# Second layer's experts: slots and gathers of the second and third unit moved ahead of ordering the experts

## The chip, the cores and the metric

The kernel runs on one core of one Trainium2 chip. The number that counts is the device time of one execution in microseconds. Before the change it is 1020.47 us, the median of three runs (1019.87 to 1021.63).

The core has five instruction queues that run side by side and wait for each other through semaphores. PE is the matmul engine (TensorE), DVE the vector engine, ACT the scalar engine, POOL the GpSimd engine. SP issues most of the transfers from the chip's memory (HBM). Each queue runs its instructions strictly in the order in which they stand.

## The reference, cut to what matters

Two layers over 256 latent tokens of width 1024, with 256 context tokens beside them in the first. Each layer ends in a mixture of 16 experts, of which every token takes two, chosen within one of four groups:

```
out = zeros
for e in range(16):
    hid = silu(h @ w_gate[e]) * (h @ w_up[e])      # 1024 -> 512
    out = out + combine[:, e] * (hid @ w_down[e])  # 512 -> 1024
h = h + m[5] * out
```

The change touches only the experts of the second layer, the last part of the program. There each expert's three matrices are 2 MB each in fp32, and all 16 experts' weights are read: 96 loads of 1 MB.

## The kernel before, in words

A token goes to two experts of 16, so the kernel does not push all 256 tokens through every expert. Experts are worked through in *units*. A pair unit holds two experts with 64 slots each, a solo unit one expert with 128 slots. In the second layer `PLAN[1] = "PPSPSPPPP"`: nine units, of which the first, second, fourth and the last four are pairs. In a pair the two experts' matmuls run in two halves of the array's columns in plain fp32 (`L919`); a solo unit's weights are split into a high and a low part (`whi` on ACT, `L171`; `wlo` on DVE or POOL, `L175`) and multiplied in three products (`L504` to `L506`).

`FIXED[1] = 5`: the first five experts keep their places, and they fill units 1, 2 and 3. The other eleven are put in order of how many tokens chose them. `order` (`L946` on) counts tokens per expert, makes the permutation `perm`, and writes `ids`, the experts' numbers in their new order. SP reads these into registers (`L296`) before it can load weights of the experts with open places. `arrange` (`L970` on) then permutes the tokens' ranks and weights with small PE transposes and products (`L976` to `L994`).

Three steps make the input of a unit:

- `slots1(n)`: DVE compares the ranks of tokens with slot numbers (`sgm`, `L1606`), PE multiplies this with token numbers and weights (`L1610`), and DVE reads from the product the tokens' numbers (`sli`, `L1612`, `L1614`) and weights (`slw`, `L1618`).
- `gather1(n)`: POOL starts an indirect DMA (`L1624`) that fetches the rows of these tokens from memory into `xg`. Two buffers exist (tag `H1`). They are also the buffers of `f`, the normalised tokens; the first gather can overwrite one only after all its readers are through.
- `xpose1(n)`: PE transposes `xg` (`L1638`) into PSUM, ACT and DVE copy it into `xh` (`L1644`). For the first unit alone there is no gather: PE multiplies `f` with the slots (`L1641`).

Then come `gu("g")` and `gu("u")`, 16 matmuls each for a pair unit, `hidden`, `hid_T` (`L1020`), `down1` (16 more) and `combine1` (`L1667`). In the code before, `slots1(0)` and the first unit's input come first, then `order`, the first gate products, `arrange`, the slots and gathers of units 2 and 3, and then the loop over the units.

Weights come through a ring: at this stage 13 buffers of 1 MB. A load goes out when its buffer is free: after the last matmul on it in a pair unit, after its split in a solo unit. SP issues all loads from one queue, in a fixed order, so a load that waits holds up those behind it. The order of loads is gate of unit n, down of unit n-1, up of unit n.

PSUM tiles of the tag `tr` (transposes, slot products, small products) have two buffers, so each new one waits for the readers of the one before the last.

The order of instructions on each engine is not the order of the code. A list scheduler with a timeline model of its own places them, so an edit in one place can move instructions that it does not name, also far behind it. The readings of the order below are from the built programs.

Of the kernel before, what the change touches and what calls it, by code (L numbers as in the profile page):

```python
# [24 lines left out]
FIXED = (2, 5)  # L25
# [182 lines left out]
def backbone(ctx: ExitStack, tc: tile.TileContext, I, out):  # L208
# [19 lines left out]
    def tr_t():  # L228
        return psum.tile([128, 512], F32, name="tr", tag="tr", bufs=2)
# [278 lines left out]
    def split(hi, lo, x, eng):  # L508
        i = S.activation(hi, x, AF.Copy)  # L509
        eng.tensor_sub(lo, x, hi.bitcast(F32))  # L510
        return i
# [435 lines left out]
    def order(l, pool, nch, oh):  # L947

        pk = tr_t()
        for c in range(nch):  # L950
            T.matmul(pk[0:16, 0:16], one[:, 0:16], oh[:, c], start=(c == 0), stop=(c == nch - 1))
        t16 = lambda n, name: pool.tile([16, n], F32, name=name, tag=name)
        key, kd, kc, place, over, cap = t16(16, "key"), t16(16, "kd"), t16(1, "kc"), t16(1, "place"), t16(1, "over"), t16(1, "cap")
        V.scalar_tensor_tensor(key, pk[0:16, 0:16], 32.0, kb[l], op0=OP.mult, op1=OP.add)
        V.tensor_mul(kd, key, idt[0:16, 0:16])
        V.tensor_reduce(kc, kd, axis=AX.X, op=OP.add)
        V.tensor_scalar(kd, key, kc, None, op0=OP.is_ge)
        V.tensor_reduce(place, kd, axis=AX.X, op=OP.add)
        perm = t16(16, "perm")
        V.tensor_scalar(perm, ior[0:16, 0:16], place, None, op0=OP.is_equal)  # L960
        pt = tr_t()
        T.matmul(pt[0:1, 0:16], eid[0:16], perm, start=True, stop=True)
        V.tensor_copy(ids[l], pt[0:1, 0:16])
        V.tensor_mul(kd, perm, caps[l])
        V.tensor_reduce(cap, kd, axis=AX.X, op=OP.add)
        V.tensor_scalar(over, kc, kbe[l], 1.0 / 32, op0=OP.subtract, op1=OP.mult)
        V.tensor_sub(over, over, cap)
        return perm, cap, over
# [125 lines left out]
    with phase("moe0") as mp:  # L1094
# [17 lines left out]
        def id_weights(name, cw, n):  # L1112

            t = mp.tile([128, 4, n, 4], F32R, name=name)
            for j in (0, 3):
                V.tensor_copy(t[:, :, :, j], idk[:, :, None].to_broadcast([128, 4, n]))
            V.tensor_copy(t[:, :, :, 1], cw[:, :, 0:n])
            V.tensor_sub(t[:, :, :, 2], cw[:, :, 0:n], t[:, :, :, 1].bitcast(F32))
            return t

        ranks, idw = pm, id_weights("idw2", comb, 2)
        units = UNITS[0]
# [187 lines left out]
    with phase("odd") as op:  # L1310
# [190 lines left out]
        units = [(b, c) for b in range(2) for c in range(4)]  # L1501
# [78 lines left out]
    with phase("moe1") as mp:  # L1580
# [5 lines left out]
        units = UNITS[1]  # L1586
# [12 lines left out]
        def slots1(n):  # L1599

            u = units[n]
            w = 128 // len(u)
            sg = mp.tile([128, 2, 128], F32, name="sgm", tag="sgm", bufs=2)
            for c in range(2):
                for h, p in enumerate(u):
                    V.tensor_scalar(sg[:, c, h * w:h * w + w], ior[:, 0:w], ranks[:, c, p:p + 1], None, op0=OP.is_equal)  # L1606
            pw_ = tr_t()
            m = 2 * len(u)
            for c in range(2):
                T.matmul(pw_[:, 0:m], sg[:, c], idw[:, c, u[0]:u[0] + len(u)].rearrange("p e j -> p (e j)"),  # L1610
                         start=(c == 0), stop=(c == 1))
            V.tensor_scalar(sli[0:w, n:n + 1], pw_[0:w, 1:2], OFF, None, op0=OP.add)  # L1612
            if len(u) == 2:
                V.tensor_scalar(sli[w:128, n:n + 1], pw_[w:128, 3:4], OFF, None, op0=OP.add)  # L1614
            t = mp.tile([128, 1], F32, name="slw1", tag="slw1", bufs=4)
            for h in range(len(u)):
                hs = slice(h * w, h * w + w)
                V.tensor_copy(t[hs], pw_[hs, 2 * h:2 * h + 1])  # L1618
            slw[n] = t
            return sg  # L1620

        def gather1(n):
            xg[n] = cp.tile([128, D], F32, name=f"xg{n}", tag="H1", bufs=2)
            return G.indirect_dma_start(out=xg[n], out_offset=None, in_=fd1,  # L1624
                                        in_offset=bass.IndirectOffsetOnAxis(ap=sli[:, n:n + 1], axis=0),
                                        bounds_check=255, oob_is_err=False)

        def xpose1(n, sg=None):

            xh = mp.tile([128, KD, 128], F32R, name="xh1", tag="xh", bufs=2)  # L1630
            xl = mp.tile([128, KD, 128], F32R, name="xl1", tag="xl", bufs=1) if len(units[n]) == 1 else None
            for hf in range(2):
                pt = tr_t()
                for q in range(4):
                    ks = slice((hf * 4 + q) * 128, (hf * 4 + q) * 128 + 128)
                    o = pt[:, q * 128:(q + 1) * 128]
                    if sg is None:
                        T.transpose(o, xg[n][:, ks], idt)  # L1638
                    else:
                        for c in range(2):  # L1640
                            T.matmul(o, f1[c][:, ks], sg[:, c], start=(c == 0), stop=(c == 1))  # L1641
                fs = slice(hf * 4, hf * 4 + 4)
                if xl is None:
                    (V.tensor_copy if hf else S.copy)(xh[:, fs].bitcast(F32).rearrange("p k t -> p (k t)"), pt)  # L1644
                else:
                    split(xh[:, fs], xl[:, fs], pt.rearrange("p (k t) -> p k t", k=4), V)
            xT[n] = (xh, xl)
# [23 lines left out]
        st.more(1, lambda: Two(x_t("wa", "X"), x_t("wb", "X")))  # L1671
        st.load()
        idw = id_weights(comb)
        xpose1(0, slots1(0))
        perm, cap, over = order(1, mp, 2, oh)
        st.limit = st.upto = 1 << 30
        st.load()
# [1 line left out]
        pg = gu("g", 1, 0, *xT[0])  # L1679
        ranks, combS, ranksT = arrange(1, mp, 2, perm, pm, comb, "amt")  # L1680
        idw = id_weights(combS)
        for n in (1, 2):
            slots1(n)
            gather1(n)
        reg = any_over(mp, over)
# [137 lines left out]
```

## Time and profile before

| what | us |
|---|---|
| median of three runs | 1020.47 |
| profiled execution | 1022.2 |
| its span, first to last instruction | 1020.4 |
| PE busy in the span | 943.5 |
| DVE, POOL, ACT busy | 538.9, 351.0, 342.2 |

In the span PE works 92% of the time, at a mean granted clock of 0.963 of full speed. The second layer's experts take from about 737 us to the end. The profile's page cuts the span into 40 slices; in the last nine the transfers move between 326 and 387 GB/s, except in the very last. Just ahead of them stand slices with less (250 and 157). A listing of instructions in order of time has: start, duration, engine, line, operation, output and inputs, tiles used on PE, shape, count, and in brackets how long the engine sat idle before it and what ended this. Two records of PE stand for one fp32 matmul instruction.

### The profile page before, as it was taken

Reading aid. Unit: us, or ns where it says so; the run is one execution under the profiler, and the core shown is the slowest. Engines: PE = TensorE matmul, PEld = TensorE weight load, DVE = VectorE, ACT = ScalarE, POOL = GpSimd, SP = SyncE. Lnnn points to the kernel's source line nnn. Section 1 sums busy time; section 2 is a strip of 40 time slices with the busy share of each in tenths; the row PEclk is TensorE's granted clock in tenths of the full one; section 3 lists DMA queues with packets and bytes.
Section 4 is the critical chain, followed back from the end, with each engine's and each line's share of the span. In section 5 each row is a group of like instructions: output and inputs, shape, how many; then the busy total and the mean of one; then the engine's idle time right before and its main releaser. Section 6 shows DMA issues by size and latency. Waiting matters only on the chain. (4 is left out here: it accounts for less than half of the span.)

```text
span 1020.4 us, 12766 instructions
## 1 busy us (share of the span) xinstructions
PE 943.5 (92%) x4686; PEld 589.3 (58%) x4686; DVE 538.9 (53%) x931; ACT 342.2 (34%) x492; POOL 351.0 (34%) x244
## 2 busy tenths in 40 slices
PE   4999999988899999999999798999796999999995
PEld 2677677746675678558756577466553444643331
DVE  3552425286783777457935683648523464532223
ACT  3421113144563266236534362433201132410001
POOL 2351103235552746524823533023001242443112
PEclk9999999998899999999999999899985999999998
DMA  9964668948699799799599772495496899999993
GB/s 311 363 241 145 213 254 296 350 166 291 217 320 375 248 344 356 251 359 387 203 385 384 255 266 86 123 335 182 157 346 250 326 387 383 387 382 386 386 386 130
DMA packets 149316, 296.28 MB, mean 290 GB/s; under 512 B 6776, under 2 KB 17032, under 8 KB 149112
## 3 DMA queue, kind: packets, MB, share of 16 engines
q1 hardware_dynamic: 143080, 278.06, 76.3%
q0 software_dynamic: 6128, 17.26, 4.6%
q8 instruction: 40, 0.66, 0.3%
q14 instruction: 36, 0.29, 0.1%
q10 hardware_dynamic: 32, 0.01, 0.0%
HBM read 295.97 MB, written 4.24 MB: 294 GB/s over the span
## 5 line engine op out<-in xcount | busy, mean ns | idle before, releaser
L171 ACT ACTIVATE whi<-w 128x1024 fp32r<-128x1024 f32 x182 | 190.6, 1058 | 225.8 <-PE mm L506 93.2
L175 POOL TENSOR_TENSOR wlo<-w,whi 128x1024 fp32r<-128x1024 f32 x64 | 163.5, 2555 | 260.7 <-ACT whi L171 218.4
L175 DVE TENSOR_TENSOR wlo<-w,whi 128x1024 fp32r<-128x1024 f32 x118 | 178.4, 1524 | 95.8 <-ACT whi L171 94.9
L919 PE MATMUL mm<-w,xh 128*64 128x512 f32 x632 | 162.9, 607 | 0.5 <-DMA w<-in_moe_w_up_dram 0.5
L515 POOL TENSOR_TENSOR H<-H,am 128x512 f32<-128x512 f32 x68 | 95.6, 1423 | 146.9 <-DVE am L514 144.5
L919 PEld LDWEIGHTS mm<-w,xh 128*64 128x64 f32 x632 | 48.7, 139 | 90.9 <-issue 87.4
L504 PE MATMUL mm<-whi,xh 128*128 128x512 f32 x192 | 79.6, 414 | 2.4 <-DVE am L514 1.6
L505 PE MATMUL mm<-wlo,xh 128*128 128x512 f32 x192 | 78.8, 410 | 2.7 <-DVE wlo L175 2.3
L506 PE MATMUL mm<-whi,xl 128*128 128x512 f32 x192 | 78.0, 406 | 0.0
L919 PE MATMUL yp<-w,hh 128*64 128x512 f32 x288 | 74.0, 606 | 0.8 <-DVE hh L1023 0.8
L514 DVE TENSOR_TENSOR am<-mm,m5b 128x512 f32<-128x512 f32 x68 | 45.7, 684 | 30.6 <-PE mm L1221 19.5
L1221 PE MATMUL mm<-y,seT 128*128 128x512 f32 x208 | 54.5, 397 | 0.2 <-ACT y L509 0.2
L504 PE MATMUL mm<-aTh,whi 128*128 128x512 f32 x128 | 52.4, 416 | 2.1 <-ACT aTh L665 2.1
L505 PE MATMUL mm<-aTl,whi 128*128 128x512 f32 x128 | 51.7, 404 | 0.0
L506 PE MATMUL mm<-aTh,wlo 128*128 128x512 f32 x128 | 51.3, 402 | 0.0
L1221 PEld LDWEIGHTS mm<-y,seT 128*128 128x128 f32 x208 | 38.1, 188 | 15.4 <-issue 4.9
L919 PEld LDWEIGHTS yp<-w,hh 128*64 128x64 f32 x288 | 23.0, 140 | 41.0 <-issue 39.4
L504 PEld LDWEIGHTS mm<-whi,xh 128*128 128x128 f32 x192 | 37.4, 195 | 14.6 <-issue 4.7
L505 PEld LDWEIGHTS mm<-wlo,xh 128*128 128x128 f32 x192 | 37.5, 195 | 14.4 <-DVE wlo L175 3.4
L432 PE MATMUL yp<-w,sT 128*32 128x512 f32 x288 | 45.2, 642 | 0.0
L506 PEld LDWEIGHTS mm<-whi,xl 128*128 128x128 f32 x192 | 37.5, 195 | 7.8 <-DVE xl L510 0.3
L510 DVE TENSOR_TENSOR yl<-yp,yh 128x512 fp32r<-128x512 f32 x16 | 11.0, 690 | 58.4 <-ACT yh L509 58.4
(362 smaller groups left out, 1546.3 us busy)
## 6 DMA issues: line engine op xcount, KB each, us to landing
w<-in_moe_w_gate_dram SPq DMA_DIRECT2D x61, 1024.0 KB
w<-in_moe_w_up_dram SPq DMA_DIRECT2D x58, 1024.0 KB
w<-in_moe_w_down_dram SPq DMA_DIRECT2D x57, 1024.0 KB
w<-in_ada_w_dram SPq DMA_DIRECT2D x48, 1024.0 KB
w<-in_even_w_in_dram SPq DMA_DIRECT2D x8, 1024.0 KB
w<-in_odd_w_in_dram SPq DMA_DIRECT2D x5, 1024.0 KB
w<-in_even_w_out_dram SPq DMA_DIRECT2D x4, 1024.0 KB
s4b<-mrow SPq DMA_DIRECT2D x6, 512.0 KB
```

Of the source, the lines that this page charges most:

```text
L171: self.nc.scalar.activation(hi, t, AF.Copy)
L175: eng.tensor_sub(lo, t, hi.bitcast(F32))
L432: T.matmul(pa[32 * j:32 * j + 32, :], s_at(s * 4 + j, u), t[:, j, :], start=first and s == 0, stop=last and s == 1, skip_group_check=True)
L504: T.matmul(o, lh, rh, start=first, stop=False)
L505: T.matmul(o, lh, rl, start=False, stop=False)
L506: T.matmul(o, ll, rh, start=False, stop=last)
L510: eng.tensor_sub(lo, x, hi.bitcast(F32))
L514: V.tensor_mul(t, pp, m)
L515: eng.tensor_add(acc, acc, t)
L919: T.matmul(o[hs], xh[:, kk, hs].bitcast(F32), w[h][:, k], start=first and k == 0, stop=last and k == 3, skip_group_check=True)
L1221: marks["comb"] = T.matmul(pp, seT[n][:, c * 128:(c + 1) * 128], t[:, hs], start=(i == 0), stop=(i == 2 * len(ns) - 1))
```

## The change

The slots of unit 2 are computed right after those of unit 1, ahead of the first unit's transposed input; its gather follows that input. Slots and gather of unit 3 come next. Both take the ranks as they are before the permutation (`pm`, `comb`), which for experts with fixed places are the same numbers. Only then come `order`, the first gate products and `arrange`. Units 2 and 3 are left out of the later loop, which has nothing more to do here. `FIXED[1]` is 5 and unit 3 ends with expert 4, so `ahead` is `[1, 2]`.

```diff
         idw = id_weights(comb)
-        xpose1(0, slots1(0))
+
+        ahead = [n for n in (1, 2) if units[n][-1] < FIXED[1]]
+        sg0 = slots1(0)
+        slots1(1)
+        xpose1(0, sg0)
+        gather1(1)
+        for n in ahead[1:]:
+            slots1(n)
+            gather1(n)
         perm, cap, over = order(1, mp, 2, oh)
         st.limit = st.upto = 1 << 30
         st.load()
...
         ranks, combS, ranksT = arrange(1, mp, 2, perm, pm, comb, "amt")
         idw = id_weights(combS)
-        for n in (1, 2):
+        for n in range(1 + len(ahead), 3):
             slots1(n)
             gather1(n)
         reg = any_over(mp, over)
```

In the built program the order differs from the start of this stage on, and there are no more and no fewer instructions of these steps. First place, PE at the stage's start: the slot products (`L1610`) and the first unit's input (`L1641`); `f_6203` and `f_6320` are the two halves of the tokens.

```order
-L1610 MATMUL tr<-idw_6431,sgm 128x4
+L1610 MATMUL tr<-idw_6431,sgm 128x4 x4
 L1641 MATMUL tr<-sgm,f_6203 128x128
-L1610 MATMUL tr<-idw_6431,sgm 128x4
 L1641 MATMUL tr<-sgm,f_6320 128x128
 L1641 MATMUL tr<-sgm,f_6203 128x128
```

Unit 2's two slot products now stand ahead of the first unit's input, which waits for DVE's reading of unit 1's product; unit 3's two stand behind that input, ahead of the first gate matmul. Second place, PE between the last up product of unit 1 and the first gate product of unit 2 (`L980` to `L994` are `arrange`, `L1034` and `L1007` the overflow flag and the ranks' transposes, `L1638` the transposed input of unit 2):

```order
 L980 MATMUL tr<-perm,pmT 128x16 x2
 L985 MATMUL tr<-idt,comb 16x128 x2
 L990 MATMUL tr<-perm,cbT 128x16 x2
 L994 MATMUL tr<-pmT,perm 16x256
-L1610 MATMUL tr<-idw_6540,sgm 128x4 x2
-L1610 MATMUL tr<-idw_6540,sgm 128x2 x2
 L1034 MATMUL tr<-idt,over 1x16
 L1007 MATMUL tr<-pmST,idt 64x256 x2
-L1638 MATMUL tr<-idt,xg_6556 128x128 x8
-L1610 MATMUL tr<-idw_6540,sgm 128x4 x2
+L1638 MATMUL tr<-idt,xg_6481 128x128 x8
+L1610 MATMUL tr<-idw_6570,sgm 128x4 x2
```

Four slot matmuls are gone from here; the two of unit 4, which need the permuted ranks, still stand between unit 2's input and its first gate matmul. On ACT, in the same place, the copy of unit 2's input now comes ahead of the split of unit 3's first gate weights, and the second split further back:

```order
 L1013 ACTIVATE sg<-mm 128x512
-L171 ACTIVATE whi<-w 128x1024 x2
 L1644 COPY xh_6646<-tr 128x512
 L171 ACTIVATE whi<-w 128x1024 x2
 L1013 ACTIVATE sg<-mm 128x512
-L509 ACTIVATE yh_6708<-yp 128x512 x2
+L509 ACTIVATE yh_6708<-yp 128x512
+L171 ACTIVATE whi<-w 128x1024 x2
+L509 ACTIVATE yh_6708<-yp 128x512
```

The copy no longer stands behind work that waits for a transfer. DVE has the same turn: its copy of that input now precedes the low parts `wlo`. Third place, SP: the loads that follow the first load of unit 3's gate, before the change,

```order
L142 DMA w<-in_moe_w_gate_dram 128x4x512 [waits DMAHW2_49,DMAHW1_49,DVE_49]
L142 DMA w<-in_moe_w_down_dram 128x4x512 [waits DMAHW2_49,DMAHW3_49,DVE_49,Pool_49]
L142 DMA w<-in_moe_w_down_dram 128x4x512 [waits DMAHW4_49,PE_49]
L142 DMA w<-in_moe_w_down_dram 128x4x512 [waits DMAHW5_49,PE_49]
L142 DMA w<-in_moe_w_down_dram 128x4x512 [waits DMAHW6_49,PE_49]
L142 DMA w<-in_moe_w_up_dram 128x4x512 [waits DMAHW7_49,PE_49]
```

and now:

```order
L142 DMA w<-in_moe_w_down_dram 128x4x512 [waits DMAHW2_49,PE_49]
L142 DMA w<-in_moe_w_down_dram 128x4x512 [waits DMAHW3_49,PE_49]
L142 DMA w<-in_moe_w_down_dram 128x4x512 [waits DMAHW4_49,PE_49]
L142 DMA w<-in_moe_w_gate_dram 128x4x512 [waits DMAHW5_49,DMAHW1_49,DVE_49]
L142 DMA w<-in_moe_w_up_dram 128x4x512 [waits DMAHW6_49,PE_49]
L142 DMA w<-in_moe_w_down_dram 128x4x512 [waits DMAHW7_49,PE_49]
```

Three of unit 2's down loads, which wait for PE (the first two for the first half of unit 2's gate products, the third for their second half), now stand ahead of unit 3's second gate load, which waits for the split of its first one (the DVE semaphore); the fourth down load no longer waits for a split. Ten of the eleven register reads of `ids` and that of the overflow flag stand right ahead of these loads in one run; before, they were spread between loads. Behind this, SP's order is soon the same again. Later on PE differs in places as well: unit 3's down products now stand inside unit 4's up products, unit 4's down products come earlier within unit 5's up products, and in the last unit two of the four final combining matmuls (`L1722` before, `L1730` now) stand inside the last down products.

## Rows read from the trace of the kernel before

**Rows 1.** Busy time of each engine in stretches, with granted clock, DMA share, GB/s.

```profile
core 0: us, PE busy (x) PEld busy (x) DVE busy (x) ACT busy (x) POOL busy (x), PEclk, DMA share, GB/s
775.00:780.00 5.00, 1.94 (x8) 1.56 (x8) 0.00 (x0) 0.14 (x1) 0.00 (x0) 0.50 0.67 244
780.00:785.00 5.00, 2.61 (x8) 1.46 (x10) 3.96 (x10) 2.34 (x3) 0.11 (x1) 0.50 0.08 22
785.00:790.00 5.00, 5.00 (x18) 1.50 (x16) 0.28 (x2) 1.53 (x2) 1.22 (x2) 0.62 0.70 263
790.00:795.00 5.00, 5.00 (x25) 1.84 (x22) 2.59 (x1) 0.48 (x1) 2.02 (x1) 1.00 0.12 14
795.00:1000.00 205.00, 197.31 (x886) 91.15 (x886) 83.13 (x125) 40.58 (x56) 64.47 (x44) 0.98 1.04 386
...
1001.00:1002.00 1.00, 1.00 (x8) 0.34 (x6) 0.00 (x0) 0.00 (x0) 0.00 (x0) 1.00 0.15 55
```

**Rows 2.** PE in order of time at the stage's start.

```profile
742.29 0.77 PE L1641 MATMUL tr<-sgm,f 128*128 128x128 f32 x2
742.86 0.43 PE L1610 MATMUL tr<-idw,sgm 128*128 128x4 f32 x2
...
765.44 0.61 PE L980 MATMUL tr<-perm,pmT 16*128 16x16 f32 x4
...
766.87 0.61 PE L990 MATMUL tr<-perm,cbT 16*128 16x16 f32 x4 [0.51 <-DVE cbT L987]
...
768.70 1.84 PE L1610 MATMUL tr<-idw,sgm 128*128 128x4 f32 x8 [0.69 <-DVE idw L1595]
...
771.59 1.12 PE L1007 MATMUL tr<-pmST,idt 16*64 16x256 f32 x4 [0.85 <-DVE ovs L1036]
777.51 1.94 PE L1638 MATMUL tr<-idt,xg 128*128 128x128 f32 x8 [4.81 <-DMA xg<-fd,sli]
782.39 1.01 PE L1610 MATMUL tr<-idw,sgm 128*128 128x4 f32 x4 [2.94 <-ACT xh L1644]
783.34 12.37 PE L919 MATMUL mm<-w,xh 128*64 128x512 f32 x42
```

**Rows 3.** POOL in order of time: the first of the gathers.

```profile
770.85 1.13 POOL L1624 DMA_INDIRECT xg<-fd,sli  x1 [32.51 <-PE tr L1034]
```

**Rows 4.** SP in order of time, two rows of its loads.

```profile
783.34 0.38 SPq L142 DMA_DIRECT2D w<-in_moe_w_gate_dram  x1
793.17 2.93 SPq L142 DMA_DIRECT2D w<-in_moe_w_down_dram  x4
```

**Rows 5.** DVE in order of time: compares of unit 1's slots, and a cast of `arrange`.

```profile
741.31 0.74 DVE L1606 TENSOR_SCALAR sgm<-cst,posm 128x64 f32<-128x64 f32 x4
...
768.05 0.41 DVE L996 CAST pmST<-tr 16x256 fp32r<-16x256 f32 x1
```

**Rows 6.** ACT in order of time: the copy of unit 2's input.

```profile
781.77 0.57 ACT L1644 COPY xh<-tr 128x512 f32<-128x512 f32 x1
```

**Rows 7.** PE later in the stage: unit 3's slots and first wait; unit 4's gate.

```profile
811.91 0.50 PE L1610 MATMUL tr<-idw,sgm 128*128 128x2 f32 x4
...
821.58 0.50 PE L505 MATMUL mm<-wlo,xh 128*128 128x512 f32 x1 [2.32 <-DVE wlo L175]
...
839.07 9.66 PE L919 MATMUL mm<-w,xh 128*64 128x512 f32 x42
```

**Rows 8.** The stretches of 1 us in which the granted clock changes.

```profile
768.00:769.00 1.00, 0.31 (x3) 0.33 (x2) 0.50 (x2) 0.00 (x0) 0.00 (x0) 0.68 1.03 381
...
788.00:789.00 1.00, 1.00 (x4) 0.24 (x2) 0.00 (x0) 0.53 (x1) 0.00 (x0) 0.58 0.62 246
```

**Rows 9.** PE in order of time: the last down products and what follows.

```profile
999.32 7.09 PE L919 MATMUL yp<-w,hh 128*64 128x512 f32 x32 [0.78 <-DVE hh L1023]
1006.34 3.70 PE L1722 MATMUL mm<-yb,sgT 128*128 128x512 f32 x8
```

**Rows 10.** DVE in order of time at the end.

```profile
1003.02 0.69 DVE L1719 TENSOR_TENSOR yb<-yp,m5b 128x512 f32<-128x512 f32 x1 [3.76 <-PE yp L919]
...
1010.87 1.72 DVE L1713 TENSOR_TENSOR hg<-H,gfb 128x512 f32<-128x512 f32 x1
```

## The prediction

> **What bounds the kernel now.** I read the busy time by stretches first, because a share over the whole span hides stages. From 795 to 1000 us PE is busy for 197.31 of 205 us and the transfers run at 386 GB/s [rows 1]: PE and the weight stream are both nearly full, and the loop over the units has little room. Just ahead of it stands a hole in both. From 775 to 795 us the transfers move 244, 22, 263 and 14 GB/s [rows 1]; against 386 that is (142 + 364 + 123 + 372)/386 x 5 = 13.0 us of stream time lost. Second, PE in order of time tells why [rows 2]. Unit 1's up products end where the first row of `arrange` begins, at 765.44. Unit 2's gate begins at 783.34. In these 17.9 us PE does small products and waits: 4.81 us for unit 2's gathered rows, 2.94 us for the copy of its input. The gather was issued at 770.85 [rows 3], 5.4 us after PE had run out of matmuls, because its slots stood behind `arrange`. Third, SP [rows 4]: one gate load of unit 3 at 783.34, nothing until 793.17. So PE's gap, and the loads tied to it, are what this change can reach. At the end the stream is through in the stretch 1001 to 1002 (55 GB/s [rows 1]), while the second half of the last down products, which needs the last load, starts at 999.32 + 7.09/2 = 1002.9 [rows 9]. PE sets the end, and the stream has only about 1.9 us in hand.
>
> **The head: +1.3 us.** Unit 2's slots now stand ahead of unit 1's input. DVE does four more compares (0.74 us [rows 5]). PE runs its slot product of 0.43 us at once, but unit 1's first input product, which before started at 742.29 beside this [rows 2], takes over the PSUM buffer of unit 1's slots and must wait until DVE has read them. That reading started only when PE had done the second slot product at 742.86 + 0.43 = 743.29; now it can start when the compares are done, near 742.8, and its four tiny reads take about 0.7 us (an estimate from the 0.74 us for four compares). So the input starts near 743.55, 1.26 later, less the 0.43 us that no longer stand inside it. Behind it come unit 3's two slot products, 0.50 us at full clock [rows 7]. 1.26 - 0.43 + 0.50 = 1.3. Bounds: 0.5 if only the two products count; 2.5 if they run at half clock (0.86) and the clock's rise moves back by a microsecond too. Unit 1's 32 matmuls follow back to back; `order`'s three products only stand at other places between them. Its chain on DVE has 16 matmuls as cover and needs a tenth of that.
>
> **The gap: -10.8 us.** What is left between 765.44 and unit 2's gate, with the old durations. `arrange` ends at 768.70 - 0.69 = 768.01, as before. `L1007` needs the cast `pmST`, through at 768.05 + 0.41 = 768.46 [rows 5]; it takes 1.12, to 769.6. The transposes of unit 2's input are next, 1.94, to 771.55: their gather now goes out when unit 1's input has been read (sixteen matmuls from 743.55, at 0.43 each like the slot product: 750.4) and has 19 us, where it took 777.51 - 770.85 = 6.66 [rows 2, 3]. The wait of 2.94 goes too. ACT copied that input at 781.77 [rows 6], behind the splits of unit 3's weights, which wait for a transfer. Now the copy stands ahead of them, and its 0.57 us lie beside the second half of the transposes (0.97). Unit 4's slots add 0.95 (783.34 - 782.39). Gate 2 starts at 772.5: the gap is 7.1 instead of 17.9. Bounds: 9 us, if copies and semaphores cost 2 us more than these rows show; 5.5, if it all runs at full clock (the half-clock durations 1.12, 1.94 and 0.95 then nearly halve). I take 7.1, whose rows are the nearest. What is late next is `arrange`, whose result unit 4's slots need.
>
> **The clock: -1.4 us.** The granted clock falls in the stretch from 768 and comes back in that from 788 [rows 8]; in between it is 0.50, 1.2 GHz. Unit 2's 42 records take 12.37 us then, and 9.66 at full clock in unit 4 [rows 2, 7], so half clock costs 2.7 there. Before the fall PE had only the gaps of 0.51 and 0.69 us [rows 2], which stay; before the rise it had worked without a break from 782.39. In the changed kernel PE is at work without a break from `L1007` on, about 4 us ahead of gate 2, so I expect a fall and a rise inside unit 2, and take half: 1.4, bounds 0 and 2.7.
>
> The Trainium skill (TensorE: Matmul & The Clock Gate, HAM oscillation) lets the half rate come back when PE sits idle for long, as in waits for transfers. By that rule the short gaps that stay would keep the full rate, and both terms would be at their best. The trace disagrees so far: the clock fell at 768 after gaps of 0.51 and 0.69 us.
>
> **The weight stream: 0.** Were PE alone ahead, the stream would catch it. It shifts too. Unit 2's down loads wait for PE, gate 2's first half, no longer behind two splits in a row. Unit 3's first gate load is the last of eight; it landed near 778, where the stream went dry (244 of 386 GB/s fill 3.2 of the 5 us from 775), and lands no later now, since the gathers' two times 0.5 MB have moved out of its way. Gate 2 starts at 772.5 + 1.3 = 773.8. Its first half is 16 of the 42 records, 3.7 us at full clock and twice that at half: 777.5 to 781.2. First data come 1.3 us after an issue (22 GB/s from 780 to 785 is 0.3 us' worth, behind the issue at 783.34). So the hole is 1 to 4.5 us instead of 13, and the gain of 8.5 to 12, with the 1.9 in hand, covers PE's 10.9 but for half a microsecond at worst. The eleven register reads on SP lie in the same wait: they cost nothing unless they take over 10 us.
>
> **The end: +1.0 us.** Two of the last four combining matmuls, 3.70/4 = 0.925 each [rows 9], now stand inside the last down products, one matmul into their second half. They need `yb`, ready at 1003.02 + 0.69 = 1003.71 [rows 10], when PE is at 1003.3: 0.4 wait and 1.85 work. The last down product then ends 2.25 later; its `yb` (0.69) and two matmuls (1.85) follow, where before all but 0.1 of `yb` was covered and four matmuls stood (3.70). 2.25 + 0.6 + 1.85 - 3.70 = +1.0 for the last matmul. DVE's last product, 1.72 where its like take 0.69 [rows 10], may shrink: bounds 0 and 1.3.
>
> **The middle: 0.** Unit 3's and unit 4's products are interleaved otherwise. The nearest row is PE's wait of 2.32 for a low part [rows 7]; two such, gained or lost, bound it at 4.6 both ways. I find none that the new order makes certain.
>
> Sum: +1.3 - 10.8 - 1.4 + 1.0 = -9.9. Made against the profiled execution, 1022.2 us with 1.8 around its span of 1020.4, this is 1012.3; the median of the runs lies 1.7 below that execution, so I predict 1010.6.
>
> **Rivals.** *The clock holds through the gap*: 5.5 instead of 7.1, 2.7 instead of 1.4, head 1.0: 1.0 - 12.4 - 2.7 + 1.0 = -13.1, 1007.4. For it: PE's pauses shrink from 10 us to about 1. Against it: the fall at 768 came ahead of the long waits.
>
> *The stream takes over*: the hole stays at 8 us, because gate 2's first half comes at half clock and SP's reads and second-gate load add to it. Then the stream gains 5.0, the 1.9 in hand makes 6.9, the end costs 1.0: -5.9, 1014.6. For it: 386 GB/s over 205 us leaves nothing to catch up with. Against it: only the first two loads need PE's first half, and at 1.05 MB each they bridge the next 5.4 us.
>
> *It does not do what it says*: unit 4's slots still need `arrange`, and they stand ahead of gate 2. If that chain were what ends last, the gap would stay and head and end cost 2.3; with half of the two long waits left (3.9) it comes out at 1018.9. Against it: `arrange` ended at 768.01, 9.5 us before the gather came.
>
> *Slower*: unit 3's second gate load now stands behind three loads that wait for PE. It would go out near 785 (783.34 before), while unit 3 is due 10.9 us earlier, at 801.5 (its slots ended at 812.4 [rows 7]). From that issue to the next load, which waited for the split, it took 9.8 us [rows 4]; with two loads of 2.7 ahead its split ends near 800. From 801.5 on each microsecond costs at most one, and past 812 the kernel is slower; that takes four more loads ahead of it, or a split stuck as long on ACT behind unit 1's down outputs. Price: 1024.
>
> **How the numbers follow.** Forecast 0.60, clock holds 0.12, stream 0.18, no gain 0.05, slower 0.05. A difference under 0.2% (2 us) could not be told from none. The first three are all faster: 0.90; same 0.05; slower 0.05. The forecast's own bounds, head +1.2, gap +1.9, clock +1.4 and the middle, which partly cancel, give 1007 to 1014. The range reaches a little past the clock's case and past the stream's: 1006.0 to 1015.8.
>
> **What would show it.** Right: unit 2's transposes without a wait for the gather; its gate about 7 us after unit 1's up products end; the copy ahead of the splits; transfers below 300 GB/s for under 5 us between 770 and 795; the span's end near 1010.5. Wrong: a new wait of several microseconds at unit 2's input or unit 3's second half, transfers dry past 785, or PE waiting for loads in the last units.

## The result, and the profile after the change

The changed kernel took 1014.45 us (median of 13 runs, 1009.77 to 1019.41) beside 1021.42 us for the kernel before (13 runs). The ratio is 0.9939, with a 95% interval of 0.9921 to 0.9956: 6.2 us faster, 4.5 to 8.1. The forecast was 9.9 us faster and 1010.6 us. The direction was right and the time lies in the range; the forecast gain was 3.7 us too large.

The profiled execution took 1016.73 us, with a span of 1014.9. Its last stage starts 2.14 us later than in the profile before (first product at 742.18, before at 740.04). Nothing of the change stands ahead of that place, so I compare times from the stage's start. First PE in order of time, against [rows 2]:

```profile
744.01 1.84 PE L1610 MATMUL tr<-idw,sgm 128*128 128x4 f32 x8 [0.83 <-DVE sgm L1606]
745.85 5.83 PE L1641 MATMUL tr<-sgm,f 128*128 128x128 f32 x32
751.51 0.51 PE L1610 MATMUL tr<-idw,sgm 128*128 128x2 f32 x4
751.95 6.22 PE L919 MATMUL mm<-w,xh 128*64 128x512 f32 x26
...
767.62 0.61 PE L980 MATMUL tr<-perm,pmT 16*128 16x16 f32 x4
...
769.05 0.61 PE L990 MATMUL tr<-perm,cbT 16*128 16x16 f32 x4 [0.50 <-DVE cbT L987]
...
770.70 1.11 PE L1007 MATMUL tr<-pmST,idt 16*64 16x256 f32 x4 [0.34 <-DVE pmST L996]
771.75 1.97 PE L1638 MATMUL tr<-idt,xg 128*128 128x128 f32 x8
773.53 1.02 PE L1610 MATMUL tr<-idw,sgm 128*128 128x4 f32 x4
774.48 11.08 PE L919 MATMUL mm<-w,xh 128*64 128x512 f32 x42
```

The gap from `L980` to unit 2's gate is 774.48 - 767.62 = 6.86 us, where it was 17.90. The transposes (`L1638`) and the product behind them carry no bracket: neither the gathered rows nor the copy are waited for. ACT's copy now stands ahead of the split that waits for a transfer:

```profile
772.90 0.58 ACT L1644 COPY xh<-tr 128x512 f32<-128x512 f32 x1 [8.94 <-PE tr L1638]
783.32 2.01 ACT L171 ACTIVATE whi<-w 128x1024 fp32r<-128x1024 f32 x2 [9.83 <-DMA w<-in_moe_w_gate_dram]
```

Next the same kernel in stretches (columns as in [rows 1]), with the place where its transfers now slacken and the end of the stream:

```profile
775.00:780.00 5.00, 5.00 (x20) 1.55 (x18) 1.00 (x6) 0.00 (x0) 1.00 (x1) 0.76 1.05 385
780.00:785.00 5.00, 5.00 (x24) 1.74 (x20) 0.60 (x1) 1.69 (x2) 0.00 (x0) 1.00 0.97 349
785.00:790.00 5.00, 5.00 (x26) 1.77 (x25) 2.45 (x3) 0.92 (x2) 0.00 (x0) 1.00 0.99 345
790.00:795.00 5.00, 5.00 (x24) 1.52 (x22) 1.14 (x2) 0.00 (x0) 0.00 (x0) 1.00 1.02 367
...
885.00:890.00 5.00, 5.00 (x23) 1.66 (x22) 2.57 (x3) 3.43 (x4) 2.58 (x2) 1.00 0.91 342
890.00:895.00 5.00, 5.00 (x21) 3.68 (x21) 2.88 (x3) 2.15 (x3) 2.67 (x1) 1.00 0.50 159
...
994.00:995.00 1.00, 1.00 (x6) 0.27 (x2) 0.36 (x1) 0.00 (x0) 0.00 (x0) 1.00 0.21 78
```

The hole of 13.0 us at the stage's start has shrunk to (37 + 41 + 19)/386 x 5 = 1.3 us. A smaller one, (44 + 227)/386 x 5 = 3.5 us, has appeared at 885 to 895, where SP waits 10.1 us for the low part of a solo unit before it can issue the next load. The stream is through near 994.2; PE reads the last load from 997.30 on:

```profile
990.94 4.51 PE L919 MATMUL yp<-w,hh 128*64 128x512 f32 x18 [0.78 <-DVE hh L1023]
995.39 1.98 PE L1730 MATMUL mm<-yb,sgT 128*128 128x512 f32 x4
997.30 3.65 PE L919 MATMUL yp<-w,hh 128*64 128x512 f32 x14
1001.73 1.98 PE L1730 MATMUL mm<-yb,sgT 128*128 128x512 f32 x4 [0.78 <-DVE yb L1727]
```

So PE still sets the end. To see where the time went I cut the stage at four rows that both traces have, and summed over stretches of 1 us: idle is length less PE busy, half-clock loss is PE busy times (1 - granted clock), the rest is PE's work as it would take at full clock.

| stretch (us) | before | after | idle | half clock | rest |
|---|---|---|---|---|---|
| start to unit 1's last up product | 25.40 | 25.44 | 0.0 | 0.0 | 0.0 |
| from there to unit 2's gate (gap) | 17.90 | 6.86 | -8.95 | -1.13 | -0.96 |
| unit 2's gate and up | 18.18 | 16.89 | 0.0 | -1.30 | 0.0 |
| from there to PE's end | 208.52 | 212.34 | +0.05 | -0.45 | **+4.22** |
| behind PE's end | 10.36 | 11.19 | | | |
| sum | 280.36 | 272.72 | | | |

12.3 us were won up to unit 2's last up product. 3.8 were given back up to PE's end, and 0.8 behind it. In the 3.8 the waits are no longer in sum than before: PE was busy for 4.2 us longer with the same matmuls. That is where the missing part of the gain is, and what the experiments had to explain.

Rows of that stretch give the theory. A pair unit's two experts use two halves of the array's columns (`128*64`), and their matmuls run side by side only when neighbours in PE's queue are of different halves:

```profile
894.60 1.07 PE L919 MATMUL mm<-w,xh 128*64 128x512 f32 x2
895.60 0.50 PE L1667 MATMUL mm<-yh,sgT 128*128 128x512 f32 x1
...
898.29 3.65 PE L919 MATMUL mm<-w,xh 128*64 128x512 f32 x14
...
909.60 3.65 PE L919 MATMUL mm<-w,xh 128*64 128x512 f32 x16
...
984.15 4.51 PE L919 MATMUL mm<-w,xh 128*64 128x512 f32 x16
```

Two records are one matmul. Eight matmuls (x16) take 3.65 us. Cut into one and seven by another matmul, the one takes 1.00 us (894.60 to 895.60) and the seven again 3.65, since one of them has no neighbour either. So an odd cut costs about 0.9 to 1.0 us. Counted in the built programs (PE's order, with the half that each matmul uses), 14 of 336 pair matmuls stand alone before and 18 after. In the traces, where partners start less than 0.05 us apart, 14 and 20 run alone. The two more are in the last row: a matmul starts at 984.15, its partner's load lands at 984.97, and the partner starts at 985.01. So a wait inside a pair cuts like another instruction does, and the eight take 4.51 us. Past unit 2 the traces have 8 and 16 alone, which is 4 places more. At 0.83 to 0.93 us each (e2 and e3 below) that is 3.3 to 3.7 us of the 4.2.

### The profile page after: what moved, and what is told of

It reads as the page before. It is cut to its first block, busy times and chain, and to the rows that moved or that the text cites. A ratio compares the mean times of both kernels' runs of the same rounds, so it can differ in the third digit from the quotient of the medians.

```text
span 1014.9 us, 12758 instructions
## 1 busy us (share of the span) xinstructions
PE 946.5 (93%) x4686; PEld 590.0 (58%) x4686; DVE 539.5 (53%) x931; ACT 341.3 (34%) x492; POOL 351.2 (35%) x244
## 5 line engine op out<-in xcount | busy, mean ns | idle before, releaser
L175 DVE TENSOR_TENSOR wlo<-w,whi 128x1024 fp32r<-128x1024 f32 x118 | 181.6, 1550 | 97.8 <-ACT whi L171 96.9
## 6 DMA issues: line engine op xcount, KB each, us to landing
w<-in_odd_w_in_dram SPq DMA_DIRECT2D x5, 1024.0 KB, 14.4
```

Of the source, the lines that this page charges most:

```text
L175: eng.tensor_sub(lo, t, hi.bitcast(F32))
```

## The experiments

The stage's total (first product to the span's end) is 272.72 us in both profiles of the changed kernel; their spans differ by 2.9 us, all of it ahead of the stage. Whole runs of one kernel scatter by 10 us, so the table has both, the stage from one profile each. Each ratio is to runs of the kernel before that were made beside that kernel (their medians lie between 1020.11 and 1021.42), so ratios do not follow from the medians of the table alone. "Alone" counts pair matmuls without a partner, in PE's order and in the trace; the last three columns are sums over stretches of 1 us, as above.

| kernel | median us (runs) | ratio to before (95%) | alone (order, trace) | stage | idle | half clock | rest |
|---|---|---|---|---|---|---|---|
| before | 1021.42 (13) | 1 | 14, 14 | 280.36 | 18.3 | 12.6 | 239.1 |
| changed | 1014.45 (13) | 0.9939 (0.9921 to 0.9956) | 18, 20 | 272.72 | 9.4 | 9.8 | 242.3 |
| e1 changed, again | 1013.50 (8) | 0.9929 (0.9903 to 0.9954) | 18, 20 | 272.72 | 9.3 | 10.0 | 242.3 |
| e2 changed, paired | 1009.29 (6) | 0.9900 (0.9873 to 0.9927) | 0, 0 | 269.10 | 16.7 | 7.5 | 234.0 |
| e3 before, paired | 1019.92 (12) | 0.9982 (0.9957 to 1.0007) | 2, 2 | 279.14 | 25.4 | 10.0 | 233.5 |
| e4 tail put back | 1011.08 (6) | 0.9908 (0.9880 to 0.9936) | 16, 20 | 271.90 | 8.9 | 9.7 | 242.2 |
| e5 paired, tail | 1007.95 (6) | 0.9875 (0.9847 to 0.9902) | 0, 0 | 268.79 | 17.5 | 6.9 | 233.6 |
| e6 unit 2 only | 1009.61 (6) | 0.9901 (0.9874 to 0.9928) | 20, 20 | 271.76 | 8.0 | 9.9 | 242.7 |
| e7 late gathers | 1025.11 (10) | 1.0041 (1.0019 to 1.0062) | 16, 16 | 283.02 | 20.7 | 11.3 | 240.7 |
| e8 no split on POOL | 1011.41 (6) | 0.9915 (0.9886 to 0.9945) | 18, 22 | 269.52 | 10.4 | 6.6 | 241.5 |
| e9 changed, less load | 1012.25 (11) | 0.9922 (0.9898 to 0.9947) | 20, 20 | 271.27 | 7.5 | 9.8 | 242.7 |
| e10 e5, less load | 1002.51 (6) | 0.9838 (0.9808 to 0.9869) | 0, 0 | 261.98 | 12.2 | 6.6 | 232.3 |
| e11 e5 and e8 | 1007.96 (6) | 0.9889 (0.9859 to 0.9918) | 0, 0 | 267.98 | 15.2 | 6.9 | 234.5 |
| e12 before, copy first | 1019.09 (12) | 0.9977 (0.9952 to 1.0001) | 14, 16 | 278.68 | 15.8 | 12.4 | 240.0 |

**e1, e2 and e3: the pairs.** e1 is the changed kernel without an edit. e2 and e3 write each pair's matmuls with the second half first, in the second layer alone:

```diff
-                for h in range(2):
+                for h in ((0, 1), (1, 0))[l]:
```

> The changed kernel as it is, beside which the next three are read. From its profile and that of before: PE idle 9.0 us less and half-clock loss 2.8 less from the stage's start to PE's end, 3.3 us more of matmul time at full clock, and 0.9 more behind PE's last matmul, together 7.6 us faster at an equal start. Theory A (split pairs): the 3.3 are six more matmuls that stand alone in a half of the array's columns, so this kernel stays 5 to 9 us faster than before. Rival B (the weight stream took over): the gain was eaten by waits for loads, and the trace would show PE idle on DMA for 2 us or more; the first trace shows 0.4.

> In the second layer the second half's matmul of each pair is traced first, so that its partner can follow at once. In the order of PE no matmul of a pair unit stands alone any more: 168 slots of time for 336 matmuls instead of 177. A lone one takes 1.00 us in the trace of the changed kernel (894.60 to 895.60), as long as two side by side. Theory A: 9 slots of 0.9, so 8 us faster than the changed kernel, as far as the loads allow; the last load landed about 2.8 us ahead of its use, and a hole of 3.4 us stands in the stream from 880 to 900, so 3 to 6 us are what can come out, with PE waiting for loads in the last units. Rival C (the 3.3 us are only how the records of a trace are cut, and the order costs nothing): within 1 us of the changed kernel, and PE's matmul time at full clock as before.

> The same edit in the kernel before: 169 slots instead of 174. Theory A: 5 slots of 0.9, 4.5 us faster than before, as far as the loads allow (1.9 us in hand at the end). Rival C: within 1 us of before. If A holds, the distance between the two paired kernels is that of the early slots alone, without what the order gave back: 8 to 11 us.

By the counts of the table the kernel before has 175 places (14 alone) where the expectation says 174. The changed kernel has four more alone in PE's order and six more in the trace, as e1's expectation says. Two that run alone make one place more: e2's work fell by 242.3 - 234.0 = 8.3 us for the trace's 10 places, 0.83 us each, and e3's by 5.6 for 6, 0.93 each. Rival C is out. But only 3.6 us of the 8.3 came out in e2, and 1.2 of 5.6 in e3. In e2 PE now waits for loads; waits of PE over the stage (line, releaser, us in total, times, longest):

```profile
PE yp L919 <- DMA w<-in_moe_w_down_dram: 3.6, 2, 1.9
...
PE mm L919 <- DMA w<-in_moe_w_up_dram: 2.3, 2, 1.7
...
PE mm L919 <- DMA w<-in_moe_w_gate_dram: 1.1, 1, 1.1
```

These are 7.0 us where the changed kernel has 0.4. In e3 the gap ahead of unit 2 grows first, from 17.9 to 19.8 us: PE arrives earlier at rows that come no earlier. It also waits 3.3 us for loads later, where the kernel before has no such wait over 0.15 us. By its runs e3 can't be told from the kernel before (0.9957 to 1.0007), so its 1.2 us rest on the profile. The waits at the gap:

```profile
PE tr L1638 <- DMA xg<-fd,sli: 5.5, 1, 5.5
PE tr L1610 <- ACT xh L1644: 4.5, 1, 4.5
```

The distance between the two paired kernels is 279.14 - 269.10 = 10.0 us in the stage, close to the forecast sum, though in e2 the loads take part in it.

**e4: the tail.** Both last down products are issued first, and the combining matmuls are pinned behind them:

```diff
+        yp2 = [y_t(), y_t()]
+        for half in range(2):
+            mm_unit(yp2[half], 1, NU - 1, "d", hh, hl, 0, True, True)
         for half in range(2):
...
-            pp = y_t()
-            mm_unit(pp, 1, NU - 1, "d", hh, hl, 0, True, True)
-            V.tensor_mul(yb[:, hs], pp, m5b[:, hs])
+            V.tensor_mul(yb[:, hs], yp2[half], m5b[:, hs])
```

> In the changed kernel the four last combining matmuls stand behind all last down products again, as before the change; nothing else moves on PE. The forecast's term for the end: 1.0 us faster than the changed kernel. Theory A adds the pair that was cut in two there (0.9): 1.8 to 2.0 us faster. Rival D: the interleaving hides the first reading of the products, and this one is 0.5 to 1 us slower.

0.8 us in the stage, all of it ahead of PE's end. What follows PE's end stays at 11.2 us. The runs' intervals overlap with e1's, so this size rests on the profile. D is out. A's 1.8 is not reached: in the trace the last down products are still cut into nine and seven, by a wait of 0.42 us that it puts down to SP. So the odd cut at the end is still there, and the 0.8 is the price of the interleaving without it.

**e5: both edits together.**

> The paired kernel with the four last combining matmuls behind all last down products. In the trace of the paired kernel the last load has landed 2 us ahead of the last down products' second half, and PE waits 0.79 us twice for the products' reading at the end. Theory A (pairs and tail add): 0.8 to 2.0 us faster than the paired kernel, about 10 to 12 us faster than before. Rival B (the stream sets the end there): within 0.5 us of the paired kernel.

0.3 us in the stage, where PE now waits 7.8 us for loads: B. The medians are 1.3 us apart, with intervals that overlap.

**e6 and e7: which part of the change counts.** e6 takes `ahead = [1]`. e7 leaves the slots early and holds the gathers back:

```diff
-        gather1(1)
         for n in ahead[1:]:
             slots1(n)
-            gather1(n)
...
+        late = mp.tile([128, 1], F32, name="late", tag="late")
+        with tc.issue_after(G.tensor_tensor(late, combS[:, 1, 0:1], combS[:, 1, 0:1], op=OP.add).ins):
+            for n in ahead:
+                gather1(n)
         idw = id_weights(combS)
```

> Only unit 2's slots and gather stand ahead; unit 3's stay in the later loop. Theory A (the gain is unit 2's gathered rows and what follows them): four slot records return into the gap (0.9 us at half clock) and leave the head (0.5), so within 1 us of the changed kernel, with a gap of 7.5 to 8 us between unit 1's last up product and unit 2's first gate product (6.86 in the changed kernel, 17.90 before). Rival E (the order on POOL and SP needs both units early): the gap is 12 us or more and the time 4 us or more above the changed kernel.

> Slots of units 2 and 3 stay early, but both gathers stand on POOL behind a small addition that needs the permuted weights, so they go out near 1 us after these are ready. Theory A: unit 2's rows come 6.7 us later, PE waits about 4.8 us for them, ACT splits unit 3's weights ahead of the copy again and adds up to 2.9; the gap is 14 to 16 us, and the time 6 to 9 us above the changed kernel. Rival F (the gap was the slots' compares and products, not the rows): a gap under 10 us and at most 2 us above the changed kernel.

e6's stage is within 1 us (271.76 against 272.72), with a gap of 8.5 us: unit 3's early slots and gather bring nothing of their own. Its runs are 4 to 5 us faster than the changed kernel's by the medians, with intervals that overlap; the stage does not show that. e7 is 10.3 us slower than the changed kernel, more than expected, and its gap is 782.69 - 764.03 = 18.7 us. PE in order of time:

```profile
764.03 0.61 PE L980 MATMUL tr<-perm,pmT 16*128 16x16 f32 x4
...
774.91 1.94 PE L1638 MATMUL tr<-idt,xg 128*128 128x128 f32 x8 [6.67 <-DMA xg<-fd,sli]
781.74 1.02 PE L1610 MATMUL tr<-idw,sgm 128*128 128x4 f32 x4 [4.89 <-ACT xh L1644]
782.69 12.02 PE L919 MATMUL mm<-w,xh 128*64 128x512 f32 x42
```

Both old waits are back, and longer, though the gather goes out 3.5 us behind the `L980` row where it was 5.4 before, and PE can use the rows 10.9 us behind it instead of 12.1. ACT's copy stands behind the split of unit 3's first gate weights again, and that split, which waits for a transfer, starts at 779.22, 15.2 us behind `L980` (14.4 before). So early slots alone gain nothing: the gap hung on when the gather goes out, and on the place of the copy on ACT, which moves with it. By its runs e7 is slower than the kernel before, by 2 to 6 us.

**e8: a stall that both kernels have.** Unit 3's second low part makes PE wait 2.67 us, as it did before (2.32 [rows 7]). In e8 no low part of the second layer is made on POOL (the choice of engine in `_prep` gets `and self.key[i][:2] not in (("g", 1), ("u", 1), ("d", 1))`).

> In the second layer no low part is made on POOL; DVE makes all of them. Theory A: DVE's low part at 806.74 took 5.62 us in the changed kernel (1.21 alone) because two products of POOL run beside it; PE waits 2.67 us for it and falls to half clock behind it (2.96 us lost). Without POOL's part the wait shrinks to 1 us or less: 2 to 5 us faster than the changed kernel. Rival G (DVE becomes the bound of the solo units): new waits of PE for DVE's low parts, within 1 us of the changed kernel or up to 3 us slower.

The wait is gone and so is the half clock behind it, together 5.6 us; 3.2 came out, since waits for loads rose from 0.4 to 4.1. A holds.

**e9, e10 and e11: who sets the end.** In e9 and e10 four gate loads bring half of their rows, and the matmuls read that half twice:

```diff
+                    if (name, l) == ("g", 1) and u == UNITS[1][5]:
+                        half = lambda p=p, r0=r0, c0=c0: w[expert(l, p), r0:r0 + 256, c0:c0 + 512].rearrange("a (k p) f -> (a p) k f", p=128)
+                        st.add((name, l, p), [(lambda t: t[:, 0:2], half)], False)
+                        continue
...
-                    T.matmul(o[hs], xh[:, kk, hs].bitcast(F32), w[h][:, k], start=first and k == 0, stop=last and k == 3,
+                    T.matmul(o[hs], xh[:, kk, hs].bitcast(F32), w[h][:, k % 2 if (l, n, name) == (1, 5, "g") else k], start=first and k == 0, stop=last and k == 3,
```

> The changed kernel with the four gate loads of the sixth unit half as long (2.1 MB less, 5.4 us at 387 GB/s; the unit multiplies the first half twice, so its part of the result is another). Theory A (PE sets the end of the changed kernel): PE waits 0.4 us for loads there, so within 1 us of the changed kernel. Rival B (the stream has taken over): 3 to 5 us faster.

> The same halved gate loads of the sixth unit in the paired kernel with the tail put back; the unit's part of the result is another. There PE waits 7.8 us for loads from 930 us on. Theory A (with the pairs whole, the stream sets the end): most of these waits go, 3.5 to 5.4 us faster than the paired kernel with the tail put back. Rival C (the waits are the price of another order and would stand somewhere else): within 1 us of it.

> Pairs whole, tail put back and no low part on POOL together. PE has 3 to 5 us less to do or to wait for in the solo units than in the paired kernel with the tail put back. Theory A (the stream sets the end): within 1 us of that kernel, with more waits for loads in the last units. Rival C: 3 to 5 us faster than it.

e9 gains 1.5 us in the stage, half a microsecond more than A allows and far from B's 3 to 5. PE's order differs a little in e9: two waits of 0.84 us of the hidden values' transposes (`L1020`) for DVE (`L1014`) are missing, which alone is as much, so little of the 1.5 need come from the loads. e10 gains 6.8 against e5, more than A's 5.4, in the medians 5.4 and by the two ratios 3.8. Its waits for loads fall from 7.8 to 4.4 us, half of the 6.8; a wait of 1.2 us for a low part is gone as well, and the rest stays open. e11 adds the edit of e8, worth 5.6 us to PE there, and gains 0.8 in the stage and nothing in the runs; PE waits 7.5 us for loads in it. So PE sets the end in the changed kernel, and with the pairs whole the loads do in the main, at 386 GB/s. e5 and e11 beat both kernels, by 11 to 13 us against before. That this stage needs fewer bytes or an earlier start of the stream to get below that is a conclusion; e10 shows the first of the two.

**e12: the copy by itself.** The kernel before, with the splits of unit 3's first gate weights held behind the two copies of unit 2's input (`st.after`, `st.upto`); the order on PE, SP and POOL is that of before.

> The kernel before with one thing of the change alone: ACT and DVE copy unit 2's input ahead of the splits of unit 3's first gate weights. PE's, SP's and POOL's order is that of before, and as many pairs are cut. Theory A (the gap had two causes in a row, the gathered rows 4.81 us and the copy 2.94 us): the wait of 2.94 goes to 0 to 0.4, the gap falls from 17.9 to about 15, and the time by 2 to 3 us, with the rest of the gap left. Rival H (the copy's wait only covers another, the weights or the stream, in which before had 1.9 us in hand): the gap falls but the time by less than 1 us, with PE waiting for loads later.

```profile
765.32 0.61 PE L980 MATMUL tr<-perm,pmT 16*128 16x16 f32 x4
...
777.46 1.94 PE L1638 MATMUL tr<-idt,xg 128*128 128x128 f32 x8 [4.87 <-DMA xg<-fd,sli]
779.22 1.02 PE L1610 MATMUL tr<-idw,sgm 128*128 128x4 f32 x4
780.17 12.19 PE L919 MATMUL mm<-w,xh 128*64 128x512 f32 x42
```

The gap is 14.85 us and the stage 1.7 us shorter: the copy's wait was a cause of its own, as A says. Of the 3.05 us by which the gap fell 1.7 came out: in the trace a wait of 0.30 us, put down to SP, cuts the last down products into nine and seven, one place more than before, and the work is 0.9 us longer. By the runs alone e12 can't be told from the kernel before (0.9952 to 1.0001).

## Why the prediction was right, and where its sum was off

- **Head, +1.3: 0.0.** The input's first product starts at 745.85 - 2.14 = 743.71 (forecast 743.55), and unit 1's gate 0.70 us later than before. That is half of the term: the clock came back as far behind the stage's start as before (the stretch 747 to 748 had 0.56 before, 750 to 751 has 0.96 now), so more of the delayed input ran at full clock. The other 0.7 was returned by the order: unit 1's 64 records take 15.67 us instead of 16.33, with one place less cut.
- **Gap, -10.8: -11.0.** Right, step by step. e7 and e12 show its causes separately: the gather, and behind it the copy.
- **Clock, -1.4: -1.3.** Unit 2's 42 records take 11.08 us, between 12.37 and 9.66 [rows 2, 7]. The forecast had a fall and a rise inside unit 2; only the rise lies there, and the fall came in the gap. The rows in which the granted clock falls and comes back:

```profile
770.00:771.00 1.00, 0.66 (x4) 0.36 (x5) 0.85 (x6) 0.00 (x0) 0.00 (x0) 0.78 1.04 395
771.00:772.00 1.00, 1.00 (x5) 0.26 (x2) 0.14 (x1) 0.00 (x0) 0.00 (x0) 0.50 1.04 385
...
777.00:778.00 1.00, 1.00 (x6) 0.38 (x4) 0.00 (x0) 0.00 (x0) 0.00 (x0) 0.81 1.04 373
```

  A mean of 0.78 in the first stretch puts the fall at 770.56, inside the pause of 0.34 us ahead of 770.70 and behind one of 0.50 and small products. Before the change it fell inside the pause of 0.69 ahead of 768.70 [rows 2, 8]. The rule of the Trainium skill (TensorE: Matmul & The Clock Gate, HAM oscillation), that the half rate comes back when PE idles for long, would have kept the full clock here; the measurement decides against it. The rival built on it, a clock that holds, is out.
- **Stream, 0: about +1.2.** The hole is 1.3 us (forecast 1 to 4.5). PE waits 0.35 us for an up load at 979.67, and the other late up load cuts the pair at 984.15, 0.86 us, where the forecast allowed half a microsecond. The rival that the stream takes over is false in the main for this kernel, and true as soon as PE's order is repaired (e2, e5, e10). One premise was off: unit 3's first gate load did not land near 778 before, since ACT's split, which waits for it, starts at 779.86; now that split starts at 783.32, 1.3 us later behind the stage's start. It does no harm, because the copy no longer stands behind it.
- **End, +1.0: about +1.6.** The interleaving costs 0.8 (e4). Behind PE's last matmul another 0.8 was added that e4 does not remove. It lies between ACT's last sum and the first product of the normalisation, where the program branches (2.25 us before, 3.01 now); why it is longer stays open.
- **Middle, 0: +1.8** (3.8 in the last stretch, less the end's 0.8 and the stream's 1.2). This is the step that failed: "I find none that the new order makes certain." I looked in the moved rows for waits, and there are none. The cost is in matmul time: three more odd cuts in PE's order, which e2 and e3 price at 0.83 to 0.93 each, 2.5 to 2.8 us (one of them in the last down products, which e4 does not mend); a little less waiting and half clock gives some of that back. With the cut that the load makes, 0.5 to 0.9 of the 4.2 us of extra work stay unexplained. The order did show the cuts: seven and nine matmuls instead of eight and eight.

These terms make -7.7, and the stage -7.6; the runs (4.5 to 8.1) hold that, and not the forecast of 9.9. The median of 1014.45 is almost what the stream rival gave (1014.6), but by another cause: most of what is missing is PE's own work. That the time lies in the range owes more to the range's width than to the sum.

"Slower" is out: unit 3's second gate load went out at 786.79, and its stall was there before. "No gain" is out with the gap.

## What to carry to other kernels

When work is moved under a scheduler, count not only waits in the new order but also what now stands between instructions that only pay as neighbours: here an odd number of half-array matmuls costs as much as the next even one. A gain on one engine is worth what the next limit leaves: of 8.3 us of matmul time, 3.6 came out, because the loads had only 3 us in hand. And split a gap into its causes before moving things: here it was the time at which the gather goes out, and the place of a copy that follows from it, not the work in front of it.

## What the runs showed of the hardware that was not expected

A matmul on one half of the array's columns, without a partner, takes as long as two side by side: 0.83 to 0.93 us more per odd cut, from the work of four kernels. A wait for the second matmul's load does the same as an instruction between the two (984.15, above).

DVE's low part of unit 3 took 5.62 us where the same product takes 1.21 alone. POOL's products beside it, then DVE's own row, from the changed kernel:

```profile
806.43 2.53 POOL L515 TENSOR_TENSOR H<-H,am 128x512 f32<-128x512 f32 x2
808.92 2.35 POOL L175 TENSOR_TENSOR wlo<-w,whi 128x1024 fp32r<-128x1024 f32 x1
```

```profile
806.74 5.62 DVE L175 TENSOR_TENSOR wlo<-w,whi 128x1024 fp32r<-128x1024 f32 x1
```

POOL ends at 811.27 and DVE 1.09 us later, as if it had started only then. The Trainium skill (SBUF — State Buffer, Who interferes with whom) says that a DVE instruction with two inputs from SBUF contends with a POOL instruction that reads there. The rows agree. In e8, without POOL's part, DVE makes two low parts beside POOL's two additions in 4.30 us, still more than 2 x 1.21, and PE has no stall at this place.
